# Feed-forward by seven products: products chained in their PSUM banks, sums off GpSimd, all first products early

## The chip, the cores and the metric

The kernel runs on one core of a Trainium2 chip. The metric is the device time of one execution in microseconds, the median over several runs. The core has TensorE (PE, matmuls into PSUM banks of 512 fp32 columns), VectorE (DVE), ScalarE (ACT), GpSimd (POOL) and SyncE (SP), which here issues the DMA transfers.

## The reference

Two transformer blocks over 1024 tokens of width 1024, in fp32. The change concerns the last step of the second block, its feed-forward part and the norm behind it:

```python
h = _rms_norm(x, norm_ffn_pre[i])                              # 1024 x 1024
f = jnp.square(jax.nn.relu(h @ w_ffn_up[i])) @ w_ffn_down[i]   # 1024 -> 4096 -> 1024
x = x + _rms_norm(f, norm_ffn_post[i])
```

## The kernel before

An fp32 operand is split into hi + lo (`split`, L176: ScalarE copies the high half, L163, VectorE subtracts to get the low one, L181), and a product is three matmuls, hi·hi, hi·lo and lo·hi, summed in a PSUM bank (`mm3`, L196). Each matmul has 128 rows and 512 columns of output.

Both products of the feed-forward part are done by quarters with seven products instead of eight (Winograd's form of Strassen's algorithm). `finish` (L1505) computes the normed input as quarters B11, B21 (first half of the tokens, split) and R12, R22 (second half), and then runs `up` and `down`.

`up` (L1640) goes over 16 column tiles ct. The weights of a tile are two transfers (`load`, L1649), each with two quarters: a11, a12 and a21, a22. p1 = a11·B11, and p1 + a12·B21 is a quarter of the result; this pair is `start` (L1671 and L1673), and it is done for 8 tiles ahead, while the last steps of the attention finish and the sums T1 to T4 and B22 are fitted (L1698 to L1716, partly on GpSimd: L1714 to L1716). The tile loop (L1725) does the rest: sums of the weights on VectorE (`sums`, L1686 to L1689), five products, each into a bank of its own that is read once and freed, copies of two of them on ScalarE (L1732, L1733), sums on VectorE (L1734 to L1742) and one on GpSimd (L1736). `out` (L1664) applies relu and square on ScalarE and stores to u_d in DRAM. Tiles 8 to 15 do `start` in the loop.

`down` (L1747) goes over four groups g of the 4096, with seven products of 1024 by 512 by 512 each, every one into four banks (`product`), which VectorE adds to one of seven accumulators in SBUF (`add`, L1802). Loads are quarters of u_d and w_ffn_down by two row tiles (L1766); operands are split 512 wide. The sums are L1818 to L1823 on VectorE and L1824, L1825 on GpSimd; in the last group GpSimd adds the accumulators (L1805, L1809). Then comes the last norm, eight row tiles after another (L1851 squares on ScalarE, L1853, L1857 on GpSimd or VectorE, L172 the power on GpSimd, L1858, store L1859).

Instructions are laid into a row per engine when the program is built: a scheduler of the library orders them by a simulated timeline, so the row isn't the order of the code. On the chip every engine goes through its row in order, SP through its stores and loads as well. Tiles come from pools; a `Ring` hands out tiles of several pools in turn, and a tile waits for the readers of what lay there before.

## Time and profile before

| | us |
|---|---|
| runs of before | 2567.87, 2569.66, 2576.97 (median 2569.66) |
| profiled execution, span | 2565.9 |
| of it the feed-forward part | 1874 to 2566 |
| PE busy over the span | 2384.1 (93%) |
| DVE, ACT, POOL busy | 1557.2, 1048.5, 463.1 |

The profile is one execution. Times are microseconds from the start of the span. A row of the timeline gives start, duration, engine, line, operation, out<-in, shape, and in brackets the idle time before it and what ended it.

### The profile page before, as it was taken

The numbers are of one execution on the slowest core, as the hardware profiler recorded it, in microseconds if no ns is written. First come the engines' busy times: TensorE is split into PE (matmuls) and PEld (weight loads), VectorE is DVE, ScalarE is ACT, GpSimd is POOL, SyncE is SP. The second block draws the span as 40 slices with busy tenths as digits, with TensorE's granted clock in tenths as the row PEclk, the third lists the DMA queues.
The fourth block names the chain that finished last, engine by engine and source line by source line (L and its number), as shares of the span: only waits on it lengthen the run. The fifth ranks groups of instructions, "written<-read, shape, count | busy, mean of one in ns | idle before, by whom it ended". The sixth has DMA issues, their size and how long they took to land.

```text
span 2565.9 us, 39213 instructions
## 1 busy us (share of the span) xinstructions
PE 2384.1 (93%) x14288; PEld 2092.8 (82%) x14288; DVE 1557.2 (61%) x3370; ACT 1048.5 (41%) x2371; POOL 463.1 (18%) x772
## 2 busy tenths in 40 slices
PE   7898999999999998999998788989998999899985
PEld 6887998898887798778898688988987788688864
DVE  5432456455445545366663356757687665789899
ACT  4312344444443235333342344445565455444333
POOL 1000000000001001011103535331031100212266
PEclk9999999999999999999998899999999999999988
DMA  3134212212214532235467666534455333433303
GB/s 111 52 111 145 79 48 80 80 57 86 67 58 159 159 117 82 69 94 160 119 181 188 167 160 176 152 92 144 148 156 143 109 119 103 160 131 132 124 12 120
DMA packets 363281, 298.31 MB, mean 116 GB/s; under 512 B 126032, under 2 KB 296912, under 8 KB 363088
## 3 DMA queue, kind: packets, MB, share of 16 engines
q1 hardware_dynamic: 336976, 267.49, 34.8%
q10 hardware_dynamic: 25472, 26.22, 3.5%
q8 instruction: 112, 1.84, 0.3%
...
q14 instruction: 81, 0.66, 0.1%
...
## 4 chain that ended last, share of the span: by engine, by line
PE 70%; DVE 10%; DMA 9%; issue 4%; ACT 3%; POOL 3%; SPq 1%; ACTq 0%; DVEq 0%; POOLq 0%
PE pj L199 11%; PE pj L200 11%; PE pj L201 11%; PE pv L425 4%; PE x L199 4%; PE x L200 4%; PE x L201 4%; PE tp L253 3%; DVE w L181 3%; DMA wr<-w_ffn_up 2%; PE y L200 1%; PE Z L1313 1%; PE y L201 1%; PE y L199 1%; PE sc L685 1%
## 5 line engine op out<-in xcount | busy, mean ns | idle before, releaser
L199 PE MATMUL pj<-w,hT_hi 128*128 128x256 f32 (+2 forms) x1280 | 388.4, 308 | 14.7 <-ACT w L177 4.8
L181 DVE TENSOR_TENSOR w<-wr,w 128x512 fp32r<-128x512 f32 (+3 forms) x445 | 313.9, 740 | 142.2 <-ACT w L163 141.4
L200 PE MATMUL pj<-w,hT_hi 128*128 128x256 f32 (+2 forms) x1280 | 385.2, 302 | 0.0
L201 PE MATMUL pj<-w,hT_lo 128*128 128x256 f32 (+2 forms) x1280 | 383.9, 301 | 0.0
L163 ACT ACTIVATE w<-wr 128x512 fp32r<-128x512 f32 (+3 forms) x441 | 251.3, 617 | 226.3 <-PE x L201 67.5
L199 PEld LDWEIGHTS pj<-w,hT_hi 128*128 128x128 f32 x1280 | 245.0, 193 | 21.7 <-ACT w L177 5.2
L199 PE MATMUL pj<-hT_hi,w 128*128 128x512 f32 (+1 forms) x608 | 243.3, 401 | 8.1 <-DVE tg L829 6.3
L200 PEld LDWEIGHTS pj<-w,hT_hi 128*128 128x128 f32 x1280 | 246.2, 192 | 2.8 <-issue 1.2
L201 PEld LDWEIGHTS pj<-w,hT_lo 128*128 128x128 f32 x1280 | 246.1, 192 | 0.6 <-issue 0.5
L200 PE MATMUL pj<-hT_lo,w 128*128 128x512 f32 (+1 forms) x608 | 240.8, 396 | 0.0
L201 PE MATMUL pj<-hT_hi,w 128*128 128x512 f32 (+1 forms) x608 | 236.8, 396 | 0.0
L172 POOL TENSOR_TENSOR rstd<-rs_t,mhalf 128x1 f32<-128x1 f32 x88 | 58.8, 671 | 880.3 <-DVE rs_t L171 829.4
L199 PEld LDWEIGHTS pj<-hT_hi,w 128*128 128x128 f32 (+1 forms) x608 | 114.6, 188 | 34.3 <-ACT w L163 5.5
L201 PEld LDWEIGHTS pj<-hT_hi,w 128*128 128x128 f32 (+1 forms) x608 | 114.6, 188 | 24.4 <-issue 0.5
L200 PEld LDWEIGHTS pj<-hT_lo,w 128*128 128x128 f32 (+1 forms) x608 | 114.9, 189 | 22.9 <-issue 0.8
L402 DVE TENSOR_REDUCE mx<-sc 128x1 f32<-128x128 f32 (+7 forms) x96 | 70.9, 755 | 101.5 <-PE sc L410 101.0
L199 PE MATMUL x<-T,w 128*128 128x512 f32 x256 | 101.4, 396 | 5.6 <-DVE u L1740 3.9
L253 PE MATMUL tp<-ident,p 128*128 128x128 f32 x576 | 98.5, 278 | 8.0 <-ACT pt L163 6.9
L200 PE MATMUL x<-T,w 128*128 128x512 f32 x256 | 100.6, 393 | 0.0
L201 PE MATMUL x<-T,w 128*128 128x512 f32 x256 | 99.9, 391 | 0.0
L200 PE MATMUL y<-w 128*128 128x512 f32 x224 | 89.5, 401 | 11.1 <-DVE w L181 11.1
L201 PE MATMUL x<-w 128*128 128x512 f32 x224 | 88.1, 395 | 6.5 <-DVE w L181 6.5
...
## 6 DMA issues: line engine op xcount, KB each, us to landing
...
```

The lines of the kernel that those rows point to most:

```text
L163: self.nc.scalar.activation(out, in_, AF.Copy)
L172: nc.gpsimd.tensor_tensor(out, t, self.mhalf[:, :ss.shape[-1]], op=OP.pow)
L181: self.nc.vector.tensor_sub(lo, x, hi.bitcast(F32))
L199: mm(ps, a[0], b[0], start=first, stop=False)
L200: mm(ps, a[0], b[1], start=False, stop=False)
L201: mm(ps, a[1], b[0], start=False, stop=last)
L253: self.nc.tensor.transpose(tp[:, j * 128:j * 128 + 128], s, ident)
L402: nc.vector.tensor_reduce(mx, sc[:, :n], axis=AX, op=OP.max)
L425: self.nc.tensor.matmul(o[:, :w], pts[j], V[:, j], start=j == 0, stop=j == nb - 1)
L685: nc.tensor.matmul(o, qn, KN[:, c0:c0 + w], start=True, stop=False)
L1313: mm(ps[:, j * 128:j * 128 + 128], lhs(c), rhs(c, j), start=True, stop=True)
```

## The change

- `up`: `start` runs for all 16 tiles ahead, among the fittings; x1 and x4 are formed on VectorE. The tile loop has five products in two banks per tile: bank ua takes T2, then T3 and T4 on top of it, bank ub takes T1, then B22. VectorE reads a bank between (u2 and u3) and for the three results, o. ScalarE's copies and GpSimd's addition are gone. The weights of tiles 0 to 7 are loaded again, a11 and a12 (48 transfers, 40 before). At ct == 8 three loads of `down` are set. A pool ps6 holds the two banks twice.
- `down`: operations are 1024 wide (a pair of banks, [128, 2, 512]), with the banks y and z. Products are chained: s2·t2 and a21·b12 onto a11·b11, in the last group also s4·b22 onto the product of the sums of a11 and b11. There are five accumulators (C11, C12, C21, C22, U3) and no sums on GpSimd. Operands have 7 slots of double size. In the last group the order of products differs, C21 and C22 are normed (`last_norm`) ahead of the last product, and the rest with it.
- The number of matmuls and their shapes stay.

The diff, cut to its core (comments and docstrings, which the diff strips too, are left out):

```diff
...
-def mm3(self, ps, a, b, first, last):
-    mm = self.nc.tensor.matmul
-    mm(ps, a[0], b[0], start=first, stop=False)
-    mm(ps, a[0], b[1], start=False, stop=False)
-    mm(ps, a[1], b[0], start=False, stop=last)
+def mm3(self, ps, a, b, first, last, onto=False):
+    def mm(a, b, start, stop):
+        self.nc.tensor.matmul(ps, a, b, start=start, stop=stop, **{"skip_group_check": True} if onto else {})
+    mm(a[0], b[0], first, False)
+    mm(a[0], b[1], False, False)
+    mm(a[1], b[0], False, last)
...
-                self.slots = Ring(self.pool(st, "slots", bufs=7, side="right"), 7)
+                self.slots = Ring(self.pool(sh, "slots", bufs=5, side="right"), 5)
...
-                up = self.up(sh, sy, ep, B11, B21, R12, R22)
+                up = self.up(st, sh, sx, sy, ep, B11, B21, R12, R22)
...
-    def mul(a, x):
-        ps = self.bank("x")
+    def mul(a, x, ps=None, tag="x"):
+        first = ps is None
+        ps = self.bank(tag) if first else ps
         for k in range(4):
-            self.mul_k(ps, a[:, :, k], x[:, :, k], k == 0, k == 3)
+            self.mul_k(ps, a[:, :, k], x[:, :, k], first and k == 0, k == 3, not first)
         return ps
...
-    def start(ct, a11, a12):
-        p1 = ep.tile([128, 512], F32, name="p1")
+    def start(ct, a11, a12, p):
+        p1 = p.tile([128, 512], F32, name="p1")
...
     for ct in range(8):
-        early.append(start(ct, *load(ct, 0)))
+        early.append(start(ct, *load(ct, 0), ep))
...
+    def more():
+        ct = len(early)
+        early.append(start(ct, *load(ct, 0), ep2))
...
+        more()
         for k in ks:
             fit(B22, k, R22[:, k])
+        more()
         for k in ks:
             nc.vector.tensor_sub(R12[:, k], R12[:, k], R22[:, k])
             fit(T3, k, R12[:, k])
+            more()
...
-            nc.gpsimd.tensor_sub(x1, R22[:, k], x2)
-            nc.gpsimd.tensor_sub(x4, F(B21[:, 0, k]), x2)
-            nc.gpsimd.tensor_add(x4, F(B21[:, 1, k]), x4)
+            more()
+            nc.vector.tensor_sub(x1, R22[:, k], x2)
             fit(T1, k, x1)
+            more()
+            nc.vector.tensor_sub(x4, F(B21[:, 0, k]), x2)
+            nc.vector.tensor_add(x4, F(B21[:, 1, k]), x4)
             fit(T4, k, x4)
+    assert len(early) == 16
...
+    sx.close()
+    self.raw3 = self.pool(st, "raw3", bufs=6)
...
     up2 = self.pool(sh, "ue2", bufs=2, side="right")
+    extra = self.pool(sh, "ps6", bufs=2, space=PSUM)
+    self.psum.update(ua=extra, ub=extra)
     for ct in range(16):
-        if ct:
-            X = [load(ct, ch) for ch in range(2)]
-        p1 = early[ct] if ct < len(early) else start(ct, *X[0])
-        (a11, a12), (a21, a22) = X
-        s12, s21, s2 = sums(X, up2.tile([128, 512], F32, name="s")) if ct else ready
+        (a11, a12), (a21, a22) = [load(ct, ch) for ch in range(2)]
...
-        u2, u3, u4 = (E("u2"), E("u3"), E("u4"))
-        nc.scalar.activation(u4, mul(s12, B22), AF.Copy)
-        nc.scalar.activation(u3, mul(s21, T3), AF.Copy)
-        nc.vector.tensor_add(u2, mul(s2, T2), p1)
-        nc.vector.tensor_add(u3, u3, u2)
-        nc.gpsimd.tensor_add(u4, u4, u2)
-        p5 = mul(slot(a11), T1)
-        nc.vector.tensor_add(u2, p5, u3)
-        out(ct, 1, 1, u2)
-        nc.vector.tensor_add(u4, p5, u4)
-        out(ct, 0, 1, u4)
-        nc.vector.tensor_add(u3, mul(slot(a22), T4), u3)
-        out(ct, 1, 0, u3)
+        s, p1 = (E("s"), early[ct])
+        s4 = s.rearrange("p (k c) -> p k c", k=4)
+        nc.vector.tensor_sub(a21, a21, a11)
+        nc.vector.tensor_add(s4, a21, a22)
+        nc.vector.tensor_add(a11, a11, s4)
+        nc.vector.tensor_sub(a12, a12, s4)
+        u2, u3 = (E("u2"), E("u3"))
+        pa = mul(slot(s4), T2, tag="ua")
+        nc.vector.tensor_add(u2, pa, p1)
+        pb = mul(slot(a11), T1, tag="ub")
+        mul(slot(a21), T3, pa)
+        nc.vector.tensor_add(u3, pa, p1)
+        o = E("o")
+        nc.vector.tensor_add(o, pb, u3)
+        out(ct, 1, 1, o)
+        mul(slot(a22), T4, pa)
+        o = E("o")
+        nc.vector.tensor_add(o, pa, p1)
+        out(ct, 1, 0, o)
+        mul(slot(a12), B22, pb)
+        o = E("o")
+        nc.vector.tensor_add(o, pb, u2)
+        out(ct, 0, 1, o)
+        if ct == 8:
+            self.ahead = [self.down_load(self.raw3.tile, *x) for x in (("u", 0, 0, 0), ("d", 0, 0, 0), ("u", 0, 1, 0))]
     for x in (self.raws, self.slots):
...
 
+def down_load(self, tile, what, g, ch, h):
+    ts = []
+    for k in (0, 2):
+        t = tile([128, 2, 512], F32, name="wr")
+        cols = slice(h * 512, h * 512 + 512)
+        if what == "u":
+            src = self.u_d[ch, g * 4 + k:g * 4 + k + 2, :, cols].rearrange("k p t -> p k t")
+        else:
+            dn = self.A["w_ffn_down_2"][0].rearrange("(k p) c -> p k c", p=128)
+            src = dn[:, ch * 16 + g * 4 + k:ch * 16 + g * 4 + k + 2, cols]
+        self.nc.sync.dma_start(t, src)
+        ts.append(t)
+    return ts
...
 def down(self, st):
...
+    psum = self.pool(st, "ps7", bufs=2, space=PSUM)
+    ring, self.raws = (self.raws, Ring(self.pool(st, "raw4", bufs=13), 13))
+    self.raws.pools += ring.pools + [self.raw3] * 6
+    self.raws.i = -1
+    slots = self.pool(st, "slots3", bufs=7, side="right")
...
+    C = [fp.tile([128, 4, 2, 512], F32, name="c%d" % i) for i in range(2)]
+    U3 = fp.tile([128, 4, 512], F32, name="u3")
+    C11, C12, C21, C22 = (C[0][:, :, 0], C[0][:, :, 1], C[1][:, :, 0], C[1][:, :, 1])
...
+            w = slots.tile([128, 2, 2, 512], F32R, name="w")
+            self.split(w[:, 0], w[:, 1], t)
+            ts += [w[:, :, 0], w[:, :, 1]]
...
-    def product(a, x):
-        for t in range(4):
-            pool, tag = next(banks)
-            ps = pool.tile([128, 512], F32, name=tag, **{"bufs": 4} if tag == "x" else {})
-            for k in range(4):
-                self.mul_k(ps, a[k][:, :, t * 128:t * 128 + 128], x[k], k == 0, k == 3)
-            yield (t, ps)
+    def product(a, x, tag, into=None):
+        a, x = (split(a), split(x))
+        for i in range(2):
+            ps = into[i] if into else psum.tile([128, 2, 512], F32, name=tag)
+            for j in range(2):
+                t = i * 2 + j
+                for k in range(4):
+                    self.mul_k(ps[:, j], a[k][:, :, t * 128:t * 128 + 128], x[k], into is None and k == 0, k == 3, into is not None)
+            yield (i, ps)
...
+    def read(acc, name, g, i, ps):
+        o = acc[:, i * 2:i * 2 + 2]
+        if g == 0 and (name, i) not in first:
+            first.add((name, i))
+            self.evac(o, ps)
+        else:
+            nc.vector.tensor_add(o, ps, o)
...
+        if g == 0:
+            a11, b11, a12 = self.ahead
+            b21 = load("d", 1, 0)
...
+        run(C11, "c11", a11, b11, A_, keep="u")
+        if not last:
+            run(C11, "c11", a12, b21, B_)
+        s2, t2, s4, t4 = ([], [], a12, b21)
         if last:
+            s4, t4 = [[self.raws.tile([128, 2, 512], F32, name="wr") for _ in range(2)] for _ in range(2)]
+        for i in range(2):
+            s, x = [fp.tile([128, 2, 512], F32, name=n, bufs=2) for n in ("s", "t")]
+            nc.vector.tensor_sub(a21[i], a21[i], a11[i])
+            nc.vector.tensor_add(s, a21[i], a22[i])
+            nc.vector.tensor_sub(b12[i], b12[i], b22[i])
+            nc.vector.tensor_sub(x, b11[i], b12[i])
+            s2.append(s)
+            t2.append(x)
+        run(C12, "c12", s2, t2, A_, into="u")
+        for i in range(2):
+            nc.vector.tensor_add(a11[i], a11[i], s2[i])
+            nc.vector.tensor_sub(b11[i], b22[i], t2[i])
+            nc.vector.tensor_sub(s4[i], a12[i], s2[i])
+            nc.vector.tensor_sub(t4[i], b21[i], t2[i])
+        run(U3, "u3", a21, b12, A_, into="u")
+        run(C22, "c22", a11, b11, B_, keep="p")
+        if last:
+            for i in range(2):
+                o = slice(i * 2, i * 2 + 2)
+                nc.vector.tensor_add(C21[:, o], C21[:, o], U3[:, o])
+                nc.vector.tensor_add(C22[:, o], C22[:, o], U3[:, o])
+        run(C21, "c21", a22, t4, A_)
+        if last:
+            gp = self.raws.tile([128, D], F32, name="wr")
+            nc.sync.dma_start(gp, rows(A["norm_ffn_post_2"]))
...
-        add(0, split(a11), split(b11), (1, 0), (2, 0))
-        s, x = (split(a12), split(b21))
-        add(1, s, x)
...
-            nc.gpsimd.tensor_sub(q(b11), q(b22), x)
-            nc.gpsimd.tensor_sub(q(b21), q(b21), x)
...
-        add(2, s2, t2, (3, 2), (6, 2))
-        add(3, split(a21), split(b12), (5, 3), (4, 3))
...
+                self.last_norm(fp, gp, C[1][:, t], 512 + t * 128, (0, 1))
+            run(C11, "c11", a12, b21, A_)
+            done = [self.last_norm(fp, gp, C[0][:, t], t * 128, (0,)) for t in range(4)]
+            for i, ps in product(s4, b22, B_, held["p"]):
+                for j in range(2):
+                    t = i * 2 + j
+                    nc.vector.tensor_add(C12[:, t], ps[:, j], C12[:, t])
+                    self.last_norm(fp, gp, C[0][:, t], t * 128, (1,), done[t])
...
-        r0 = (half * 4 + t) * 128
+            run(C12, "c12", s4, b22, B_, into="p")
+def last_norm(self, fp, gp, x, r0, cs, done=None):
...
+        done = (x2, fp.tile([128, 2], F32, name="s2", bufs=8))
+    x2, ss = done
+    whole = len(cs) == 2
...
+    nc.scalar.activation(junk[:, :n], v[:, sl], AF.Square, accum_out=ss[:, cs[0]:cs[0] + 1])
+    nc.vector.tensor_mul(v[:, sl], v[:, sl], gp[:, sl])
+    if cs == (0,):
+        return done
...
-        r = self.norm_rows(s1, D)
-        for c in range(2):
-            sl = slice(c * 512, c * 512 + 512)
-            (nc.gpsimd if half or c == 0 else nc.vector).tensor_mul(xs[c], xs[c], gp[:, sl])
-            nc.vector.scalar_tensor_tensor(x2[:, sl], xs[c], r, x2[:, sl], op0=OP.mult, op1=OP.add)
-        nc.sync.dma_start(self.out[0, r0:r0 + 128, :], x2)
+    r = self.norm_rows(s1, D)
+    nc.vector.scalar_tensor_tensor(x2, v, r, x2, op0=OP.mult, op1=OP.add)
+    nc.sync.dma_start(self.out[0, r0:r0 + 128, :], x2)
...
```

How the change moves instructions, at three places. Names are those of the program with a number. First VectorE at the start of the tile loop: u_20962 and u_21343 are the last u of the first products, T4 is the last fitted sum, s is the sum a21 + a22, wr are loaded weights, w their split halves. Before:

```order
L1673 TENSOR_TENSOR u_20962<-x_20966,p1_20944 128x512
L1687 TENSOR_TENSOR u_20992<-wr_20990 128x512
L1688 TENSOR_TENSOR wr_20988<-wr_20988,u_20992 128x512
L1689 TENSOR_TENSOR wr_20988<-wr_20988,u_20992 128x512
L1700 TENSOR_TENSOR T4_21013<-x4_21043,T4_21013 128x1024
L181 TENSOR_TENSOR w_20997<-wr_20988,w_20997 128x512
L181 TENSOR_TENSOR w_21000<-wr_20990,w_21000 128x512
L181 TENSOR_TENSOR w_21003<-u_20992,w_21003 128x512
```

After:

```order
L1678 TENSOR_TENSOR u_21299<-x_21303,p1_21281 128x512
L1678 TENSOR_TENSOR u_21343<-x_21347,p1_21325 128x512
L1742 TENSOR_TENSOR s_21390<-wr_21388 128x512
L1742 TENSOR_TENSOR s_21495<-wr_21493 128x512
L1743 TENSOR_TENSOR wr_21386<-wr_21386,s_21390 128x512
L1744 TENSOR_TENSOR wr_21386<-wr_21386,s_21390 128x512
L1743 TENSOR_TENSOR wr_21491<-wr_21491,s_21495 128x512
L1744 TENSOR_TENSOR wr_21491<-wr_21491,s_21495 128x512
L181 TENSOR_TENSOR w_21397<-s_21390,w_21397 128x512
L181 TENSOR_TENSOR w_21414<-wr_21386,w_21414 128x512
```

The sums stood ahead of the fit of T4 before; now they stand behind the last u of the first products, and the splits behind them.

Second, ScalarE and SP at the turn from `up` to `down`: w are high halves, u3, u4 and o the last results of `up`, u_d what is stored, wr what is loaded for `down`. ScalarE before:

```order
L1666 ACTIVATE u4_23015<-u4_23015 128x512
L163 ACTIVATE w_23203<-wr_23159 128x512
L163 ACTIVATE w_23280<-wr_23165 128x512
L163 ACTIVATE w_23283<-wr_23167 128x512
L1665 ACTIVATE u3_23014<-u3_23014 128x512
L1666 ACTIVATE u3_23014<-u3_23014 128x512
L163 ACTIVATE w_23286<-wr_23167 128x512
L163 ACTIVATE f0_0_23125<-y0_23209 128x512
```

ScalarE after:

```order
L1671 ACTIVATE o_23053<-o_23053 128x512
L163 ACTIVATE w_23122<-wr_22331 128x1024
L163 ACTIVATE w_23125<-wr_22333 128x1024
L163 ACTIVATE w_23128<-wr_22335 128x1024
L163 ACTIVATE w_23131<-wr_22337 128x1024
L163 ACTIVATE w_23186<-wr_22339 128x1024
L163 ACTIVATE w_23189<-wr_22341 128x1024
L1670 ACTIVATE o_23073<-o_23073 128x512
L1671 ACTIVATE o_23073<-o_23073 128x512
L163 ACTIVATE w_23192<-wr_23102 128x1024
```

SP before:

```order
L108 DMA u_d_19089<-u2_23013 128x512
L108 DMA u_d_19089<-u4_23015 128x512
L108 DMA u_d_19089<-u3_23014 128x512
L1766 DMA wr_23171<-u_d_19089 128x2x512
L1766 DMA wr_23173<-u_d_19089 128x2x512
```

SP after:

```order
L108 DMA u_d_19089<-o_23053 128x512
L108 DMA u_d_19089<-o_23073 128x512
L1778 DMA wr_23102<-w_ffn_down_2 128x2x512
L1778 DMA wr_23104<-w_ffn_down_2 128x2x512
L1778 DMA wr_23106<-u_d_19089 128x2x512
L1778 DMA wr_23108<-u_d_19089 128x2x512
```

Six high halves of double width now stand ahead of the relu and the square of the last o_23073, whose store stands ahead of ten loads of `down` (six shown).

Third, VectorE among the sums of the last group: s, t and wr are sums of quarters, f and c the accumulators. Before:

```order
L1823 TENSOR_TENSOR t_25290<-wr_25055,wr_25075 128x512
L181 TENSOR_TENSOR w_25258<-t_25276,w_25258 128x512
L1819 TENSOR_TENSOR s_25289<-wr_25067,wr_25071 128x512
L181 TENSOR_TENSOR w_25254<-s_25275,w_25254 128x512
L1823 TENSOR_TENSOR t_25304<-wr_25055,wr_25075 128x512
L181 TENSOR_TENSOR w_25259<-t_25290,w_25259 128x512
L1820 TENSOR_TENSOR wr_25059<-wr_25059,s_25289 128x512
L1821 TENSOR_TENSOR wr_25051<-wr_25051,s_25289 128x512
L1819 TENSOR_TENSOR s_25303<-wr_25067,wr_25071 128x512
L181 TENSOR_TENSOR w_25255<-s_25289,w_25255 128x512
```

After:

```order
L181 TENSOR_TENSOR w_24607<-wr_24574,w_24607 128x1024
L181 TENSOR_TENSOR w_24610<-wr_24576,w_24610 128x1024
L1859 TENSOR_TENSOR wr_24572<-wr_24572,s_24672 128x1024
L1862 TENSOR_TENSOR wr_24670<-wr_24584,t_24673 128x1024
L1861 TENSOR_TENSOR wr_24669<-wr_24582,s_24678 128x1024
L1862 TENSOR_TENSOR wr_24671<-wr_24586,t_24679 128x1024
L1824 TENSOR_TENSOR c0_23099<-z_24394,c0_23099 128x2x512
L1859 TENSOR_TENSOR wr_24574<-wr_24574,s_24678 128x1024
L1860 TENSOR_TENSOR wr_24576<-wr_24600,t_24673 128x1024
L181 TENSOR_TENSOR w_24613<-wr_24578,w_24613 128x1024
L1824 TENSOR_TENSOR c0_23099<-z_24420,c0_23099 128x2x512
L181 TENSOR_TENSOR w_24684<-s_24672,w_24684 128x1024
```

One sum stood between splits before, 512 wide; now a block of seven sums and reads, 1024 wide, stands between two splits.

## Rows read from the trace of the kernel before

**Rows 1.** The page, busy time, share and instructions of each engine:

```profile
PE 2384.1 (93%) x14288; PEld 2092.8 (82%) x14288; DVE 1557.2 (61%) x3370; ACT 1048.5 (41%) x2371; POOL 463.1 (18%) x772
```

**Rows 2.** Table of stretches of the feed-forward part; columns in its first line:

```profile
core 0: us, PE busy (x) PEld busy (x) DVE busy (x) ACT busy (x) POOL busy (x), PEclk, DMA share, GB/s
...
1921.00:1938.00 17.00, 6.44 (x20) 4.79 (x19) 14.96 (x14) 8.08 (x14) 8.93 (x3) 0.70 0.36 102
...
1990.00:2050.00 60.00, 54.39 (x225) 42.41 (x225) 38.76 (x55) 27.67 (x52) 6.58 (x4) 0.97 0.34 106
...
2205.00:2250.00 45.00, 36.17 (x136) 27.43 (x135) 40.96 (x55) 21.45 (x39) 13.26 (x8) 0.89 0.32 111
2250.00:2450.00 200.00, 200.00 (x882) 165.31 (x882) 176.48 (x276) 84.78 (x157) 46.50 (x19) 1.00 0.37 127
2450.00:2544.00 94.00, 80.42 (x330) 63.03 (x328) 92.70 (x101) 29.41 (x62) 67.28 (x44) 0.93 0.13 46
```

**Rows 3.** Waits of TensorE, 1874 to 2566: total us, times, longest:

```profile
PE y L200 <- DVE w L181: 11.1, 8, 3.8
PE x L199 <- ACT w L163: 10.6, 1, 10.6
PE x L201 <- DVE w L181: 6.5, 2, 4.8
PE x L199 <- DVE u L1740: 4.3, 5, 1.9
```

**Rows 4.** Timeline of TensorE, around its longest gap and at its last matmul:

```profile
1921.24 0.39 PE L201 MATMUL x<-B,w 128*128 128x512 f32 x1
1932.19 0.79 PE L199 MATMUL x<-B,w 128*128 128x512 f32 x1 [10.56 <-ACT w L163]
...
1933.64 0.63 PE L200 MATMUL x<-T,w 128*128 128x512 f32 x1
1934.06 0.63 PE L201 MATMUL x<-B,w 128*128 128x512 f32 x1
...
2543.25 0.39 PE L201 MATMUL x<-w 128*128 128x512 f32 x1
```

**Rows 5.** Timeline of VectorE, operations in a row without GpSimd beside them:

```profile
1900.15 1.22 DVE L1711 TENSOR_TENSOR x<-B,R 128x1024 f32<-128x1024 f32 x1
1901.29 1.22 DVE L1700 TENSOR_TENSOR B<-R,B 128x1024 fp32r<-128x1024 f32 x1
...
2008.21 0.69 DVE L1689 TENSOR_TENSOR wr<-wr,s 128x512 f32<-128x512 f32 x1
2008.82 0.68 DVE L1734 TENSOR_TENSOR u<-x,p 128x512 f32<-128x512 f32 x1
```

**Rows 6.** Groups by line, 1874 to 2566: busy us, mean ns, idle before:

```profile
L1802 DVE TENSOR_TENSOR f<-y,f 128x512 f32<-128x512 f32 x40 | 26.4, 684 | 3.2 <-PE y L201 3.2
...
L1735 DVE TENSOR_TENSOR u<-u,u 128x512 f32<-128x512 f32 x16 | 21.9, 1372 | 0.1
...
L1700 DVE TENSOR_TENSOR T<-x,T 128x1024 fp32r<-128x1024 f32 x6 | 14.6, 2432 | 0.1
```

**Rows 7.** Timeline of VectorE, first operations after loads, and the split before:

```profile
1998.70 0.69 DVE L181 TENSOR_TENSOR w<-wr,w 128x512 fp32r<-128x512 f32 x1 [0.54 <-ACT w L163]
...
2005.67 0.69 DVE L1686 TENSOR_TENSOR wr<-wr 128x512 f32<-128x512 f32 x1 [3.58 <-DMA wr<-w_ffn_up]
...
2217.97 1.29 DVE L1818 TENSOR_TENSOR wr<-wr 128x512 f32<-128x512 f32 x2 [2.48 <-DMA wr<-u_d]
```

**Rows 8.** Timeline of SP's queue, issues of the two loads:

```profile
1999.63 0.44 SPq L1649 DMA_DIRECT2D wr<-w_ffn_up  x1
...
2213.85 1.44 SPq L1766 DMA_DIRECT2D wr<-u_d  x3
```

**Rows 9.** Timeline of ScalarE at the turn, six high halves in a row:

```profile
2206.93 3.22 ACT L163 ACTIVATE w<-wr 128x512 fp32r<-128x512 f32 x6
```

**Rows 10.** Timeline of VectorE, its last two operations:

```profile
2559.48 0.14 DVE L171 TENSOR_SCALAR rs_t<-ss 128x1 f32<-128x1 f32 x1
2560.34 1.42 DVE L1858 SCALAR_TENSOR_TENSOR wr<-f,rstd,wr 128x512 f32<-128x512 f32 x2 [0.73 <-POOL rstd L172]
```

128 lines of the change are left out of this document (41 added, 87 removed).

## The prediction

> **What bounds the kernel now.** I read the page's busy shares first: TensorE is busy for most of the whole span [rows 1], so a change that keeps every matmul can only win back time in which TensorE stands. The diff touches the feed-forward part alone, from 1874 us (its first matmul) to the end at 2565.9; the work ahead of it is ordered as before. So the second view is the table of stretches [rows 2]. In 2250:2450 the reader sees 882 matmuls in 200.00 us, 0.227 each: TensorE never stands. For the other stretches I subtract 0.227 times the matmuls: 1921:1938 17.0 − 20 × 0.227 = 12.5 us lost, 1990:2050 9.0, 2205:2250 14.2, 2450:2544 19.2. Together 54.9 us; the stretches left out (1874:1921, 1938:1990, 2050:2205) show PE busy all the time at clock 1.00. Behind the last matmul, which starts at 2543.25 and ends at 2543.64 [rows 4], stand 22.3 us more without TensorE. So the part can win at most 77 us of its 692.
>
> The third view, TensorE's waits [rows 3], says who is late: the low halves of operands that VectorE splits (L181), ScalarE's high half once for 10.6, and VectorE's reads of PSUM for a little. The fourth shows what a stop costs [rows 4]: after the 10.56 us gap the matmuls start 0.43 apart instead of 0.227, for 9 of them, with a granted clock of 0.70 in that stretch [rows 2] (below the upper level of 2.4 GHz). That is 9 × 0.2 = 1.8 us. I add 2 to a long stop, and up to 2.4 to the longest of the down part, where the stretches' clock of 0.89 and 0.93 speaks of more than one such fall.
>
> **The work that moves.** Matmuls: 2688 of 512 columns before and after, so nothing is saved on TensorE itself. A 512-wide VectorE operation takes 0.69 and the next starts 0.60 later, a 1024-wide one 1.14 later [rows 5]. GpSimd's sums disappear, except the small powers of the norm. What they cost shows in VectorE's groups [rows 6]: L1700 T<-x, run beside GpSimd's sums, takes 2.43 instead of 1.22, and L1735, 512 wide, 1.37 instead of 0.69, while L1802, which has one operand in PSUM, stays at 0.68.
>
> The Trainium skill (SBUF — State Buffer, Who interferes with whom) says that a VectorE instruction with two SBUF inputs contends with a GpSimd instruction that reads SBUF, and one with at most one SBUF input does not. The trace agrees: 2.43 and 1.37 for two SBUF inputs, 0.68 for one. By that rule every stretched sum and split of the part goes back to its short length; that is rival (a).
>
> **Up, first products.** All 16 tiles, not 8, get their two first products beside the fitting of T1 to T4. 32 products of 12 matmuls are 87 us of TensorE with VectorE well ahead, and the sums x1 and x4 moved from GpSimd to VectorE are six 1024-wide operations, 6.8 us, hidden under it; if that cover were gone, they would cost 6.8. So the 12.5 us stop goes. What is late next is the start of the tile loop: its tile s lies where B21 lay, so its sums wait for the last early product. VectorE's order from there is u_21343, two L1742, two L1743 and two L1744, then the split w_21397: 8 × 0.60 and about 1.0 for the start and the hand-over, 5.8 us; eight matmuls that need only the high half fill 1.8 of it. Cost 4.0 and 2 for the clock: **6.0**.
>
> **Up, tile loop.** Per tile five products (60 × 0.227 = 13.6 us) against 14 VectorE operations (8.4 us). ScalarE's copies and GpSimd's additions are gone, and with them the waits of 1990:2050. The weights are loaded again for tiles 0 to 7, 48 loads instead of 40. The tightest loop is a load buffer's: VectorE's last split of a tile frees it at 1999.4 [rows 7], the load is issued at 1999.63 [rows 8] and its first user starts at 2005.67 [rows 7], 6.3 us after the buffer came free; then 11 operations × 0.60 until the last split frees it again, 12.9 us, under 13.6 by 0.7. I cost it at nothing; without that cover see rival (b). Chaining adds a wait: a product added onto a bank must follow VectorE's read of it. In the order two products (5.2 us) lie between for every tile but the last, where T4 follows T3 directly: **1.2** us (the PSUM wait rows are 4.3 us for 5, and 1.9 at most [rows 3]).
>
> The Trainium skill (PSUM — Partial Sum Buffer, Summary: rules for kernel authors) says: read PSUM while a matmul runs only from a different bank, guarded by a semaphore. It speaks against this change, since 48 add-ons in the loop meet a reader in their own bank; by it, where the read isn't done in time, TensorE stands. Rival (c) gives what the rows make of that.
>
> **Turn from up to down.** Before, 14.2 us. After, ScalarE's six 1024-wide high halves stand ahead of the last relu and square in its order, the last store waits for these on SP, and ten loads of down stand behind that store. Six 512-wide copies in a row took 3.22 [rows 9], so six of double width about 6.3, and the loads are issued from about 7 us after up's last matmul. Before, the first such load was issued at 2213.85 [rows 8] and used at 2217.97 [rows 7], 4.1 us. The first product has its loads ahead and waits only for the splits: 3.8 us and 2 for the clock. The second waits 0.3. The third needs s2 and t2, and VectorE has 31 operations of 1.14 between up's last read and its last split: 35.3 us and some 3 for start, high half and hand-over, against 25.9 by when TensorE is through with two products. Stop 12.3 to 13.2, and 2.2 for the clock. Together about **21.5**, 7 more than before.
>
> **Down.** Per group of seven products VectorE has 58 operations of 1024, 58 × 1.14 = 66 of 76.2 us; per product 4 splits and 2 reads, 6.8, so 4.06 of the 10.9 us are left for sums, three and a half of them. Sums come in clusters of five to eight: a cluster of S sums makes the splits late by 1.14 × S − 4.06, and since only seven slots exist, a split can't run far ahead. With the orders as they are, group 1's end loses about 1, group 2 3.5, group 3 1.5 and 3, the last group 9.0 (eight sums among the splits, 8 × 1.14 − 4.06 = 5.1, 1.5 carried over, 2.4 of clock), its last product 1.2; some hide each other: **17**. Whether a 1024-wide read over two banks also takes 1.14 no row shows. The nearest is the 512-wide read [rows 6], at 0.68 the same as an operation on SBUF alone, so I take 1.14; the ends are 1.14 and twice 1.22, 2.45.
>
> **End.** The last product is s4·b22, and half the rows were normed before it. Behind its last matmul: 0.2 and a read 0.7, two 1024-wide row updates of the pair before, a multiplication and small ones 3.2, then as in the trace from L171 at 2559.48 to the end of the span, 6.4 [rows 10], plus a second 1024-wide update, 1.14, and a second power, 0.5, part of it beside other work. About **12.7** instead of 22.3, −9.6. GpSimd's multiplications (L1857) and half of the row tiles that were normed late are what goes; what is last next is the transfer of the last rows.
>
> **Sum.** Stops after: 6.0 + 1.2 + 21.5 + 17 = 45.7, before 54.9: −9.2. With the end −18.8. The profiled span of 2565.9 becomes 2547; the runs' median of 2569.66 is 3.8 above that span, so 2551.
>
> **Rivals.**
> (a) VectorE keeps up. Without GpSimd beside it the clusters are absorbed (SP's loads come earlier, the seven slots suffice), and the turn stays at its 14.2. Then only 6.0 + 1.2 + 14.2 and the last cluster, 9, are left, 30.4 instead of 54.9; with the end −34: 2535. For it: VectorE was kept busy 176.48 of 200 us with stretched operations and TensorE never stood [rows 2]. Against: the 31 operations of the turn, which are counted.
> (b) The tile loop is bound by the load. If a load takes a fifth longer, 7.5 instead of 6.3 (stores stand between the loads on SP), the loop is 7.5 + 6.6 = 14.1, 0.5 over TensorE's, 16 times, +8: 2559, within 0.5%. For it: the margin is only 0.7.
> (c) Slower: chaining makes TensorE wait. A read that stands on VectorE behind a sum which waits for its load comes late, and the add-on with it; decided where this lateness passes the 5.2 us of cover. At the rows' 0.86 per wait (4.3/5) 48 add-ons cost 41: 2592.
> (d) Slower too: VectorE becomes the bound of down. If the 14 two-bank reads of a group cost 2.45 each, a group is 44 × 1.14 + 14 × 2.45 = 84.5 us, 8.2 over TensorE's 76.2; four groups 33: 2584. It decides from 10.9 us of VectorE per product.
> (e) The change doesn't act: the stops only change places, 54.9 after as before, and just the end's 9.6 is won: 2560.
>
> **How the numbers follow.** Forecast 0.46, (a) 0.22, (b) 0.10, (c) 0.05, (d) 0.06, (e) 0.11. The forecast's own range is 2543 to 2561 (turn and down each ±5). The range, 2532 to 2568, leaves out (c), (d) and some of the low side of (a). About 0.5%, 13 us, is what a measurement of this kernel can tell from no change: faster is under 2556.8, slower over 2582.5. Faster: (a) and 0.40 of the forecast, with 0.04 of (b) and (e), 0.66. Slower: (c), most of (d), 0.10. Same: the rest, 0.24.
>
> **What would show it.** In the profile after: no stop in the first products; one of 4 us at the first L1743; none within the tile loop and PE spacing of 0.227 there (L1741 waiting for a load with PE idle would be (b), L199 on ua or ub waiting for L1747 or L1750 (c)); a stop of some 12 us before the third product of down, with L1854 and L181 on VectorE's side; 1024-wide L1824 at 1.2 us (2.4 would be (d)); some 17 us in stops on w L181 over the four groups, most before the last group's fifth product; 12.7 us behind the last matmul. The prediction is wrong if the turn's 31 operations aren't in one row on VectorE, or if the load loop of up isn't under 13.6 us.

## The result, and the profile after

The changed kernel takes 2541.89 us (median of 4 runs, 2538.74 to 2545.12) against 2571.85 for the kernel before (4 runs); the ratio is 0.9872, 95% interval 0.9855 to 0.9889. Measured again beside three other kernels it took 2544.94 against 2572.0, ratio 0.9895 (0.9868 to 0.9922). The prediction was 2551, range 2532 to 2568: faster, inside the range, 9 us too high. The profiled execution's span is 2536.5 us, 29.4 below before's.

The table of stretches of the changed kernel, to be read like [rows 2] (PE busy and its matmuls, the other engines, granted clock, DMA):

```profile
core 0: us, PE busy (x) PEld busy (x) DVE busy (x) ACT busy (x) POOL busy (x), PEclk, DMA share, GB/s
1871.00:1962.00 91.00, 89.66 (x412) 74.20 (x410) 65.22 (x90) 60.57 (x98) 3.21 (x7) 1.00 0.57 172
1962.00:1970.00 8.00, 6.77 (x22) 4.81 (x23) 6.54 (x12) 3.98 (x8) 0.00 (x0) 0.79 0.96 310
1970.00:2190.00 220.00, 215.30 (x940) 174.96 (x938) 132.85 (x208) 96.86 (x168) 0.00 (x0) 1.00 0.42 129
2190.00:2233.00 43.00, 30.60 (x110) 23.42 (x109) 37.01 (x33) 16.73 (x18) 0.00 (x0) 0.81 0.48 171
2233.00:2440.00 207.00, 205.05 (x899) 168.09 (x898) 170.78 (x150) 74.85 (x77) 0.00 (x0) 1.00 0.34 112
2440.00:2452.00 12.00, 8.03 (x28) 5.76 (x28) 12.00 (x11) 3.48 (x4) 0.00 (x0) 0.86 0.00 0
2452.00:2523.00 71.00, 69.97 (x309) 57.59 (x308) 58.10 (x58) 29.07 (x41) 5.94 (x4) 1.00 0.25 89
```

As in the prediction, each matmul counts 0.227 us (0.2268, to be exact: 200.00/882 in [rows 2]) and the rest of a stretch is lost: 8 − 22 × 0.2268 = 3.0 us in 1962:1970 (and 1.3 just ahead of it), 6.8 in the tile loop (1970:2190), 18.0 in the turn (2190:2233), 3.1, 5.7 and 0.9 in the groups of down. POOL reads 0.00 from 1962 to 2452, where before it had 4.8 to 67 us per stretch; what is left of it is the small powers of the norms.

TensorE's waits from the turn on, to be read like [rows 3]:

```profile
PE y L199 <- ACT w L163: 9.4, 2, 7.1
PE y L199 <- DVE w L181: 5.2, 5, 2.2
PE z L199 <- DVE c L1824: 3.7, 1, 3.7
```

And the groups that answer to [rows 6], VectorE in down and in the fitting (L1695 is L1700 of before):

```profile
L181 DVE TENSOR_TENSOR w<-wr,w 128x1024 fp32r<-128x1024 f32 x88 | 104.0, 1219 | 29.2 <-ACT w L163 29.1
L1824 DVE TENSOR_TENSOR c<-z,c 128x1024 f32<-128x1024 f32 x22 | 26.8, 1218 | 2.3 <-PE z L199 2.3
...
L1695 DVE TENSOR_TENSOR T<-x,T 128x1024 fp32r<-128x1024 f32 x6 | 7.3, 1216 | 0.0
```

A 1024-wide read over two banks takes 1.22, as assumed, and the fit that took 2.43 takes 1.22.

**Two clocks for one comparison.** The part ahead of the feed-forward is the same in all kernels, but in the fourteen profiled executions its end, the first feed-forward matmul, came between 1869.8 and 1883.5 us (before 1874.3, the changed kernel 1869.8 and, profiled again, 1872.2). So I compare the feed-forward part by itself, from that matmul to the end of the span: 691.6 us before, 666.7 and 664.1 after. The change is worth 24.9 or 27.5 us there, and 4.5 of the 29.4 in the first pair of spans are not its own.

### The profile page after: what moved, and what is told of

The parts are those of the page before. It is cut to its first block, busy times and chain, and to the rows that moved or that the text cites. A ratio compares the mean times of both kernels' runs of the same rounds, so it can differ in the third digit from the quotient of the medians.

```text
span 2536.5 us, 38731 instructions
## 1 busy us (share of the span) xinstructions
PE 2380.1 (94%) x14288; PEld 2087.0 (82%) x14288; DVE 1495.4 (59%) x3183; ACT 1018.2 (40%) x2210; POOL 284.7 (11%) x678
## 4 chain that ended last, share of the span: by engine, by line
PE 68%; DMA 11%; DVE 9%; ACT 4%; issue 3%; POOL 3%; SPq 2%; ACTq 0%; DVEq 0%; POOLq 0%
PE pj L199 34%; PE x L199 7%; PE z L199 5%; PE y L199 4%; PE pv L426 4%; DMA wr<-w_ffn_up 3%; PE tp L254 3%; DVE w L181 2%; ACT w L163 1%; PE sc L686 1%; POOL U L1262 1%; POOL Ut L1260 1%; DMA v<-bkv_t 1%; DMA Al<-at_d 1%; PE Z L1314 1%
## 5 line engine op out<-in xcount | busy, mean ns | idle before, releaser
L199 PE MATMUL pj<-w,hT_hi 128*128 128x256 f32 (+2 forms) x2560 | 539.8, 305 | 17.6 <-ACT w L177 7.4
L199 PEld LDWEIGHTS pj<-w,hT_hi 128*128 128x128 f32 x2560 | 420.6, 192 | 27.0 <-ACT w L177 7.7
L199 PE MATMUL pj<-hT_hi,w 128*128 128x512 f32 (+1 forms) x1216 | 395.4, 400 | 10.3 <-DVE tg L830 7.2
L199 PE MATMUL pj<-w,hT_lo 128*128 128x256 f32 (+2 forms) x1280 | 383.8, 301 | 0.0
L181 DVE TENSOR_TENSOR w<-wr,w 128x1024 fp32r<-128x1024 f32 (+4 forms) x349 | 279.2, 826 | 138.8 <-ACT w L163 136.6
L163 ACT ACTIVATE w<-wr 128x1024 fp32r<-128x1024 f32 (+4 forms) x345 | 241.5, 736 | 253.4 <-PE z L199 66.4
L199 PEld LDWEIGHTS pj<-hT_hi,w 128*128 128x128 f32 (+1 forms) x1216 | 228.1, 189 | 62.5 <-ACT w L163 6.6
L199 PEld LDWEIGHTS pj<-w,hT_lo 128*128 128x128 f32 x1280 | 245.9, 192 | 0.6 <-issue 0.5
L199 PE MATMUL pj<-hT_lo,w 128*128 128x512 f32 (+1 forms) x608 | 241.9, 398 | 0.0
L199 PE MATMUL z<-w 128*128 128x512 f32 x720 | 166.9, 392 | 4.7 <-DVE c L1824 3.7
L199 PE MATMUL y<-w 128*128 128x512 f32 x624 | 150.5, 400 | 14.6 <-ACT w L163 9.4
L199 PEld LDWEIGHTS z<-w 128*128 128x128 f32 x720 | 135.7, 189 | 34.5 <-issue 4.1
L199 PEld LDWEIGHTS y<-w 128*128 128x128 f32 x624 | 119.9, 194 | 43.9 <-ACT w L163 10.7
L199 PE MATMUL ua<-T,w 128*128 128x512 f32 x576 | 139.5, 393 | 6.8 <-DVE o L1756 3.6
L199 PEld LDWEIGHTS ua<-T,w 128*128 128x128 f32 x576 | 107.3, 188 | 33.9 <-issue 8.0
L199 PEld LDWEIGHTS pj<-hT_lo,w 128*128 128x128 f32 (+1 forms) x608 | 115.4, 190 | 23.1 <-issue 0.8
L199 PE MATMUL x<-w,mix_hi 128*128 128x256 f32 x512 | 92.3, 284 | 0.0
L199 PE MATMUL x<-B,w 128*128 128x512 f32 x384 | 88.3, 390 | 0.0
```

The source lines that it names most:

```text
L163: self.nc.scalar.activation(out, in_, AF.Copy)
L181: self.nc.vector.tensor_sub(lo, x, hi.bitcast(F32))
L199: self.nc.tensor.matmul(ps, a, b, start=start, stop=stop, **({"skip_group_check": True} if onto else {}))
```

## The experiments

All kernels in one table. Each number is read from TensorE's timeline: the time of a stage less 0.2268 per matmul. Up: from its first to its last matmul (the fitting's transposes are in it, so it isn't stops alone). Turn: from there to the 145th matmul of down (three products). Groups: the rest of down. End: from the start of the last matmul to the end of the span.

| kernel | feed-forward | up | turn | groups | end | median us | ratio to before |
|---|---|---|---|---|---|---|---|
| before | 691.6 | 25.8 | 14.7 | 19.0 | 22.6 | 2571 to 2573 | |
| changed | 666.7 | 15.5 | 18.8 | 10.5 | 12.6 | 2541.9 | 0.9872 |
| changed, again | 664.1 | 14.2 | 17.9 | 10.0 | 12.6 | 2544.9 | 0.9895 |
| up_only | 682.1 | 12.5 | 21.1 | 16.8 | 22.3 | 2558.6 | 0.9951 (0.9933 to 0.9968) |
| down_only | 678.8 | 26.4 | 19.8 | 10.7 | 12.6 | 2559.0 | 0.9944 (0.9925 to 0.9962) |
| before_no_gpsimd | 664.3 | 18.3 | 10.5 | 4.3 | 21.8 | 2547.8 | 0.9903 (0.9888 to 0.9918) |
| the same again | 663.8 | 18.6 | 9.5 | 4.5 | 21.8 | 2544.0 | 0.9884 (0.9861 to 0.9908) |
| gpsimd_beside_down | 708.9 | 13.2 | 30.3 | 43.4 | 12.6 | 2590.8 | 1.0077 (1.0058 to 1.0097) |
| slots6 | 702.2 | 16.0 | 20.2 | 44.1 | 12.6 | 2581.5 | 1.0048 (1.0031 to 1.0065) |
| turn_relu_on_vector | 660.7 | 15.7 | 13.3 | 9.6 | 12.6 | 2541.1 | 0.9886 (0.9865 to 0.9908) |
| up_raws5 | 662.1 | 10.8 | 18.7 | 10.6 | 12.6 | 2543.2 | 0.9893 (0.9872 to 0.9914) |
| relu_and_raws5 | 659.1 | 11.9 | 14.3 | 10.9 | 12.6 | 2541.1 | 0.9898 (0.9860 to 0.9935) |
| the same again | 661.4 | 13.4 | 13.7 | 12.4 | 12.6 | 2539.7 | 0.9868 (0.9843 to 0.9893) |
| all_three | 660.1 | 14.2 | 14.5 | 8.4 | 13.8 | 2536.3 | 0.9855 (0.9831 to 0.9879) |

Two theories stood against each other at the start. One: the gain is what the diff's words say first, products chained in their banks, fewer operations on VectorE, early first products. The other: it is GpSimd's leaving.

**up_only**: the changed `up` with before's `down`. **down_only**: before's `up` with the changed `down`, whose three loads ahead become loads at the turn.

> The changed first product (up) with the second product and the last norm (down) of before. Theory: the gain is a sum of stops of TensorE, stage by stage, and nothing else. By the two traces up's stops fall from 12.5 + 9.0 to about 3.0 + 6.6, and the turn, the down groups and the end stay as before, so about -12 us against before, some 2560. Rival: up and down only gain together (each stage's lateness is handed on), then this one is within 5 us of before. A third: the 4.5 us by which the feed-forward part began earlier in the profiled execution of the changed kernel is of its making; then its part begins at about 1870 here too, and not near 1874.

> The first product of before, the changed second product and last norm; the three loads that the changed kernel sets ahead can't be ahead here (their buffers lie where the first product still works) and are issued at the turn. Theory: down's stops fall from 19.2 to about 10 and the end from 22.3 to 12, and the turn, 14.2 before and 18 in the changed kernel, gets worse by those loads to some 20 to 24. Together -10 to -14 us, some 2560. Rival: the down part gains by itself only what the end gives, 10 us, and loses that in the turn: within 3 us of before.

Measured 2558.6 and 2559.0. In the feed-forward part −9.5 and −12.8, together −22.3 of −24.9 or −27.5, so neither half needs the other for most of its gain. Up alone brought what its stops promised, −13.3, and lost 6.4 in the turn; down alone brought −8.3 in the groups and −10.0 at the end, and lost 5.1 in the turn. The expectation that up's turn would stay as it was fell: the first product of down waited 11.2 us (`PE y L199 <- ACT w L163`), with the first loads of w_ffn_down issued only at 2194.33, behind the last store on SP, up's last read being at 2190.85. The changed kernel has the first product's loads ahead. The third guess, that the kernel makes the feed-forward begin early, was not borne out: 1873.3 here and 1883.5 in down_only.

**before_no_gpsimd**: before, with GpSimd's sums and multiplications of `up`, `down` and the norm on VectorE, no chaining, no new order of products.

```diff
-nc.gpsimd.tensor_sub(x1, R22[:, k], x2)
+nc.vector.tensor_sub(x1, R22[:, k], x2)
...
-nc.gpsimd.tensor_add(acc[to][t], acc[to][t], acc[fr][t])
+nc.vector.tensor_add(acc[to][t], acc[to][t], acc[fr][t])
...
```

> The kernel before with every sum and multiplication of GpSimd in up, down and the last norm put on VectorE, nothing chained, widths as before. Theory (GpSimd beside VectorE costs more than its sums would on VectorE): the fitting's stop, the last group's stops and the end shrink, -10 to -20 us, and 512-wide sums on SBUF take 0.69 throughout. Rival (what matters is that chaining saves operations): VectorE takes some 70 operations more and gets later, so within 5 us of before or slower.

Measured 2547.8, ratio 0.9903, and the feed-forward part 664.3: more than expected, and as much as the whole change brings. GpSimd's additions of accumulators in the kernel before:

```profile
L1805 POOL TENSOR_TENSOR f<-f,f 128x512 f32<-128x512 f32 x24 | 39.6, 1687 | 13.9 <-DVE f L1802 13.9
```

VectorE's groups without GpSimd, with the lines of before's numbering (L1805 and L1824 were GpSimd's):

```profile
L1805 DVE TENSOR_TENSOR f<-f,f 128x512 f32<-128x512 f32 x24 | 15.0, 676 | 0.0
...
L1735 DVE TENSOR_TENSOR u<-u,u 128x512 f32<-128x512 f32 x16 | 11.0, 685 | 0.1
...
L1824 DVE TENSOR_TENSOR wr<-wr,t 128x512 f32<-128x512 f32 x16 | 10.8, 680 | 0.0
...
L1700 DVE TENSOR_TENSOR T<-x,T 128x1024 fp32r<-128x1024 f32 x6 | 7.2, 1215 | 0.0
```

The 24 additions of L1805 took 39.6 us on GpSimd and take 15.0 on VectorE, and L1700 and L1735 beside them are back at 1.22 and 0.69 from the 2.43 and 1.37 of [rows 6]. VectorE does more and is through sooner: in the feed-forward part it has 857 operations instead of 763, and is busy 526.3 us instead of 552.7. That GpSimd's sums were slow and others waited for them seems the smaller part: in the feed-forward part of before, the waits that one of its sums ended are 4.2 us in all (ScalarE's halves of T in the fitting, `ACT T L1699 <- POOL x`). Against the changed kernel the stages differ both ways: 8 us less in the turn, 6 less in the groups, 9 more at the end, 3 or 4 more in up.

**gpsimd_beside_down**: the changed kernel with GpSimd additions whose results nobody uses.

```diff
                 s2.append(s)
+                nc.gpsimd.tensor_copy(zz[0][:, :1], s[:, 0, :1])
+                for _ in range(7):
+                    nc.gpsimd.tensor_add(zz[0], zz[0], zz[1])
```

> The changed kernel with work added on GpSimd: in each of the four groups of down, two bursts of seven 512-wide additions on tiles of its own in SBUF, each burst released by a small copy of a sum; its results are not used. Theory (a VectorE operation with two operands in SBUF is held up by a GpSimd operation that reads SBUF): some 1.6 us of each addition is lost to VectorE, which has 66 of 76 us per group in use; down gets slower by 15 to 55 us, the widths' rows show splits and sums of 2.2 us and over, and L1824, with one operand in PSUM, stays at 1.22. Rival (no contention, only the number of VectorE's operations counts): no change against the changed kernel, within 5 us.

Measured 2590.8, 49 us above the changed kernel's first median, 42 in the feed-forward part, within the 15 to 55 of the theory. VectorE, ScalarE and SP have the same instructions in the same order as in the changed kernel's feed-forward part, and no wait of theirs from 2195 on is ended by GpSimd's copies or additions, so it is GpSimd's work beside them alone that costs this. VectorE by line, 2225 to 2560 (L1827 is L1824 of the changed kernel, L1866 its L1860):

```profile
L181 DVE TENSOR_TENSOR w<-wr,w 128x1024 fp32r<-128x1024 f32 x87 | 115.4, 1363 | 27.9 <-ACT w L163 27.9
L1827 DVE TENSOR_TENSOR c<-z,c 128x1024 f32<-128x1024 f32 x23 | 27.9, 1215 | 2.6 <-PE z L199 2.6
...
L1866 DVE TENSOR_TENSOR wr<-wr,t 128x1024 f32<-128x1024 f32 x8 | 16.2, 2022 | 0.0
```

The operations with two operands in SBUF get longer, the ones with one in PSUM don't. How long each waits shows in single rows, VectorE first, then GpSimd:

```profile
2308.10 1.21 DVE L1827 TENSOR_TENSOR c<-z,c 128x1024 f32<-128x1024 f32 x1
2309.23 1.43 DVE L181 TENSOR_TENSOR w<-wr,w 128x1024 fp32r<-128x1024 f32 x1
2310.58 2.29 DVE L1866 TENSOR_TENSOR wr<-wr,t 128x1024 f32<-128x1024 f32 x1
```

```profile
2308.29 1.28 POOL L1860 TENSOR_TENSOR zz<-zz,zz 128x512 f32<-128x512 f32 x1
...
2311.87 2.16 POOL L1860 TENSOR_TENSOR zz<-zz,zz 128x512 f32<-128x512 f32 x1
```

An addition of GpSimd takes 1.28 beside a read of PSUM and 2.16 beside a two-operand operation, and that one 2.29 instead of 1.21: they go in turn, a pair every 2.2 us. The addition before the last one shown runs from 2309.65 to 2311.79; VectorE's L1866, begun in the middle of it at 2310.58, ends 1.08 us behind it. The Trainium skill (SBUF — State Buffer, Who interferes with whom) calls the pair of ports that the two engines share an exclusive lock; the trace agrees, since all but 0.1 of the 1.21 us that L1866 needs alone come after the addition's end.

**slots6**: six operand slots in down instead of seven.

```diff
-slots = self.pool(st, "slots3", bufs=7, side="right")
+slots = self.pool(st, "slots3", bufs=6, side="right")
```

> The changed kernel with six operand slots in down instead of seven. Theory of the prediction: VectorE's lateness in the groups comes from too few slots, a split can't be written ahead; then six cost at least one more wait per product, and the four groups lose 20 to 50 us instead of some 10. Rival: only the clusters of sums in VectorE's row matter; the groups lose within 4 us of the same.

Measured 2581.5, the groups losing 44.1 instead of 10.5. TensorE's waits there:

```profile
PE z L199 <- DVE w L181: 15.8, 15, 3.4
PE y L199 <- DVE w L181: 13.8, 13, 3.2
```

28 waits for splits from 2230 on, one at nearly every product, where seven slots left 6 waits for `DVE w L181` from 2190 on. So the slots are the cover that the prediction took them for, and six are too few; whether more than seven would win anything, no run shows.

**turn_relu_on_vector**: the last tile's relu and square as one VectorE operation.

```diff
+if last:
+    nc.vector.scalar_tensor_tensor(u, u, 0.0, u, op0=OP.max, op1=OP.mult)
```

> The changed kernel; the relu and the square of the very last tile of up are one VectorE operation (0.7 us) instead of two on ScalarE, where they stood behind six 1024-wide copies. Theory of the turn: the ten loads behind the last store are what VectorE waits for (4.75 us of idle before L181 at 2202.60), and the third product waits for VectorE. The loads are then issued some 5 us sooner after up's last matmul and the turn loses 13 to 15 us instead of 19; the whole -4 to -5 against the changed kernel. Rival: the 31 operations of VectorE set the turn, whatever the loads do; it gains 1 us or loses 0.7.

The turn lost 13.3 instead of 18.8, as expected. SP, then VectorE, at the turn (up's last read is L1763):

```profile
2204.67 0.97 SPq L1781 DMA_DIRECT2D wr<-w_ffn_down  x2
```

```profile
2202.86 0.69 DVE L1763 TENSOR_TENSOR o<-ub,u 128x512 f32<-128x512 f32 x1 [2.03 <-PE ub L199]
2203.59 0.69 DVE L1671 SCALAR_TENSOR_TENSOR o<-o 128x512 f32<-128x512 f32 x1
2204.19 8.03 DVE L181 TENSOR_TENSOR w<-wr,w 128x1024 fp32r<-128x1024 f32 x7
```

The loads go out 1.8 us after the last read began, and VectorE runs through its splits. In the changed kernel, ScalarE, SP and VectorE:

```profile
2189.56 5.78 ACT L163 ACTIVATE w<-wr 128x1024 fp32r<-128x1024 f32 x6
2195.24 0.61 ACT L1670 ACTIVATE o<-o 128x512 f32<-128x512 f32 x1
```

```profile
2196.91 0.98 SPq L1778 DMA_DIRECT2D wr<-w_ffn_down  x2
```

```profile
2190.35 0.69 DVE L1760 TENSOR_TENSOR o<-ub,u 128x512 f32<-128x512 f32 x1 [2.03 <-PE ub L199]
2190.96 6.89 DVE L181 TENSOR_TENSOR w<-wr,w 128x1024 fp32r<-128x1024 f32 x6
2202.60 1.23 DVE L181 TENSOR_TENSOR w<-wr,w 128x1024 fp32r<-128x1024 f32 x1 [4.75 <-ACT w L163]
```

6.6 us from the read to the loads, and the 4.75 us that VectorE then stands is what the edit takes away. The feed-forward part is 6.0 us shorter than in the changed kernel's first profile, 3.4 than in its second; the −4 to −5 expected of the whole doesn't show in the median, 2541.1 against 2541.9. The profiled execution began the feed-forward at 1882.1, 12 us later than the changed kernel's; of the other executions there is no trace.

**up_raws5**: five weight buffers in the tile loop. **relu_and_raws5**: both edits.

```diff
-raws, slots = self.pool(sh, "raw2", bufs=2, side="right"), ...
+raws, slots = self.pool(sh, "raw2", bufs=3, side="right"), ...
```

> The changed kernel with five weight buffers in the tile loop instead of four, nothing else. Theory: the loop of a load buffer sets the tile loop where a load takes 7.5 us from issue to use (2074.89 to 2082.42) and not the 6.3 that I took; TensorE's waits for VectorE's reads of ua are its consequence, since the reads stand behind a sum that waits for its load. The loop's 227 us fall to 220 to 222. Rival: the chained reads themselves cost this (a bank is free only when it was read), and the loop stays within 2 us.

> Both edits, the last relu on VectorE and five weight buffers. If both theories hold the two add up: -9 to -11 us against the changed kernel, some 2532; if only one holds, its part.

Taken as a whole the loop (from its first matmul to its last) doesn't settle it: it fell from 227.1 to 222.4 us, but with both edits it was 223.6 and, again, 225.0, and 225.3 in all_three below, while four buffers gave 227.1, 227.3, 227.3, 225.9, 224.7 and in up_only 223.7. VectorE waited 37.0 and 42.8 us for `w_ffn_up` with five buffers and 45.1 or 43.2 with four; that wait is there in both.

By tiles (60 matmuls each, less 0.2268 per matmul) the traces do tell the two apart. From the seventh tile to the fifteenth the six profiles with four buffers lose 4.8, 2.4, 3.5, 1.9, 3.2 and 3.0 us (changed, changed again, up_only, gpsimd_beside_down, slots6, turn_relu_on_vector), and the four with five buffers nothing. In the first six tiles four buffers lose 1.6 to 5.7 and five 3.8 to 6.8, and the last tile loses 1.1 in all ten. So a fifth buffer ends the stops of the later tiles, and VectorE's waits for its loads, which stay, then stop TensorE no more; the first tiles hide that gain in the total. The edit also lets the scheduler order VectorE's row anew in places, and no run parts the two.

The last four kernels ran side by side, five rounds each: the changed kernel, relu_and_raws5 and before_no_gpsimd again, and **all_three**, relu_and_raws5 with 14 slots of 512 columns in place of seven of 1024.

> The changed kernel once more, beside the three others on the same chip. The part ahead of the feed-forward is the same program in all kernels, yet in the profiled executions so far the feed-forward began between 1870 and 1884 us. Theory: that is chance of an execution; then this one begins near the middle, 1878, its time is some -26 to -30 against before, and its feed-forward part again takes 667. Rival: the changed kernel begins early by itself; then it begins at 1870 again.

> The two edits together once more, beside the changed kernel. By the two traces the feed-forward part takes 659 us instead of 667; so some -8 us against the changed kernel in the median. Rival: what a stage gains is taken back in time that the profile of one execution doesn't show; then within 3 us of it.

> The two edits and 14 operand slots of 512 columns in place of seven of 1024, the same memory, splits 512 wide. Theory (a slot comes free too late, as six slots showed): slots of half the size are handed back in finer steps, and the last group's stops, 8 us, fall to 3 to 5, while VectorE pays 28 more operations per group (1.7 us of 76): -3 to -5 us against the two edits. Rival: the clusters of sums alone set them; then the same or 1 to 3 us slower by the additional operations.

> The kernel before with GpSimd's sums and multiplications on VectorE, beside the changed kernel on the same chip. By its trace its feed-forward part takes 664 us, the changed kernel's 667, before's 692. If so, it is within 5 us of the changed kernel, and taking the sums off GpSimd is by itself worth as much as the whole change. Rival: the chaining and the early products bring 10 us or more beyond it.

2544.9, 2539.7, 2536.3 and 2544.0. The changed kernel's feed-forward part took 664.1 where 667 was expected, and began at 1872.2, nearer to the rival's 1870 than to 1878; but turn_relu_on_vector and up_raws5, the same program up to there, began it at 1882.1 and 1883.1, so an early beginning isn't the kernel's own. The changed kernel and before_no_gpsimd are the same within their intervals. relu_and_raws5 is 5.3 below the changed kernel, where 8 was expected and the intervals overlap; its feed-forward part was 661.4 against 664.1. all_three has the lowest median of all, 8.7 below the changed kernel and 35.8 below before (ratio 0.9855, 0.9831 to 0.9879); the groups lost 8.4 instead of 10.9 and 12.4. Its interval overlaps those of both neighbours, so it beats before clearly and the changed kernel probably. Its theory was not borne out: the stop ahead of the last group, which it was to shorten, is still there (`PE z L199 <- DVE c L1828`, 4.2 us), and what went are stops of 0.8 to 1.4 elsewhere.

## Why the prediction was right, and where its sizes were off

- **First products: right.** 1871:1962 shows PE busy for 89.66 of 91, against a stop of 12.5 before.
- **Start of the tile loop: right, 6.0 forecast, 4.3 measured** (1.3 and 3.0), by the operations it named: TensorE waits 2.10 and 0.47 us for ScalarE's high halves, eight matmuls run on these ahead of the low halves, and the rest is the reduced clock (0.50 granted in 1964:1966).
- **Tile loop: mis-sized, 1.2 forecast, 6.8 measured** (5.1 in the second profile). The 1.2 itself was right: it stood for the last tile, where T4 follows T3 directly, and TensorE waits 0.88 us there for the read L1750, 1.1 with what is around it. The step that failed is the loop of the load buffer, costed at nothing: with four buffers it stops TensorE for most of the rest, and with five these stops are gone from the seventh tile on. That is rival (b) in its outcome, not in its reason. One load took 7.5 us from issue to first use, but the second loads of the other ten tiles around it 5.5 to 7.0, 6.0 in the mean, so the 6.3 was no bad price. Yet these loads went out every 14.3 us (2003.44 to 2146.68, ten tiles) and not every 13.6; what makes the rest of the loop longer than the 6.6 of the prediction isn't shown. The longest stop, in SP, VectorE and TensorE:

```profile
2074.89 0.38 SPq L1652 DMA_DIRECT2D wr<-w_ffn_up  x1
```

```profile
2082.42 0.69 DVE L1741 TENSOR_TENSOR wr<-wr 128x512 f32<-128x512 f32 x1 [5.04 <-DMA wr<-w_ffn_up]
...
2085.09 0.68 DVE L1756 TENSOR_TENSOR o<-ua,p 128x512 f32<-128x512 f32 x1
```

```profile
2085.92 3.01 PE L199 MATMUL ua<-T,w 128*128 128x512 f32 x12 [1.77 <-DVE o L1756]
```

The sum L1741 waits for its load, the read L1756 stands behind it on VectorE, and TensorE waits 1.77 us for the bank ua. A late read behind a sum that waits for its load is the path that rival (c) named, but L1756 is the last read of a tile's bank: what waits is a later tile's first product, not a product added onto the bank. Of the 48 add-ons one waited, the last tile's, so the chaining itself cost next to nothing in the loop.
- **Turn: right in mechanism, 21.5 forecast, 18.0 measured.** ScalarE's six copies, the loads behind the last store, a stop before the third product that ends on VectorE's side (7.14 us until ScalarE has its half of VectorE's sum t, and 2.23 until VectorE has split it). VectorE's row took as long as forecast, 38.5 us from up's last read at 2190.35 to the split with which TensorE goes on, against 38.3, but in part by luck: it is 28 operations and 5.5 us of waiting, 4.75 of it for the late loads, not 31 operations and 3. The stop came out shorter because TensorE was through with two products only after 27.8 us instead of 25.9. turn_relu_on_vector shows the loads' part in the turn, 5.5 us; of the 13.3 that it leaves, 4.2 are waits in the first product and 3.8 in the third.
- **Groups of down: mis-sized, 17 forecast, 9.7 measured.** In the groups ahead of the last the clusters cost 3.1 instead of 9.0 (1, 3.5, 1.5 and 3): I let the splits run hardly ahead, but VectorE has a lead to lose. It stands 29.1 us for ScalarE's halves, and ScalarE in turn 138.6 us, from 2241 to 2524, for TensorE to be done with a slot's last contents; slots6 shows what is lost without that lead. The last group cost 5.7 instead of 9.0, at another place and for another reason than I gave: I named late splits ahead of its fifth product, and the stop is ahead of its first. VectorE's row shows the read L1824 behind four and more sums, and TensorE starts when it is done:

```profile
2438.68 1.22 DVE L1859 TENSOR_TENSOR wr<-wr,s 128x1024 f32<-128x1024 f32 x1
2439.82 1.22 DVE L1862 TENSOR_TENSOR wr<-wr,t 128x1024 f32<-128x1024 f32 x1
2440.96 1.22 DVE L1861 TENSOR_TENSOR wr<-wr,s 128x1024 f32<-128x1024 f32 x1
2442.09 1.22 DVE L1862 TENSOR_TENSOR wr<-wr,t 128x1024 f32<-128x1024 f32 x1
2443.22 1.22 DVE L1824 TENSOR_TENSOR c<-z,c 128x1024 f32<-128x1024 f32 x1
```

```profile
2444.59 3.02 PE L199 MATMUL z<-w 128*128 128x512 f32 x7 [3.69 <-DVE c L1824]
```

It is the bank z, filled by the product just before, that was not yet read, not an operand that was not yet split.
- **End: right, 12.7 forecast, 12.2 measured** (last matmul's end at 2524.31 to 2536.5); the terms as the prediction lists them add up to 12.1, not 12.7. Neither up_only (22.3 from its last matmul's start) nor before_no_gpsimd (21.8) has it: the gain comes with down's new order (down_only has it, 12.6), half the rows normed ahead of the last product, and hardly from GpSimd's multiplications (0.8).
- **The sum.** Forecast −18.8; −24.9 in the feed-forward part. The stops I forecast as 45.7 are 38.8: the tile loop came out 5.6 higher, and the start, the turn and the groups 12.5 lower, so that the sum is off by no more than 6.9 is in part luck. The remaining 4.5 of the first pair's 29.4 came ahead of the part.
- **What the sum missed.** GpSimd had no term of its own. The prediction read the stretched widths from [rows 6], took the unstretched ones for the new kernel, and put the question of how much they bring into rival (a). before_no_gpsimd answers it: 27 us by itself, and gpsimd_beside_down shows that VectorE held up is enough to cost that much. So the words of the change, chained, early, wider, describe edits whose gains (9 to 10 us at the end, some 3 in up) and losses (8 in the turn, 6 in the groups) about cancel on top of that one. What they would bring with GpSimd's sums left in place, no run shows. Rival (a)'s condition held, VectorE being kept back by GpSimd; its place was not, since the groups of the changed kernel still lose 10 and its turn 18.

What stays open: how much of up's 15 us is stops and how much the fitting, why the load loop takes 14.3 us a tile, and why the part ahead of the feed-forward, the same program, ends 14 us apart between executions.
